# adaLN weight transfers held behind the weight stream, with other rates per stage, in a hybrid encoder block

## The chip, the cores and the metric

The kernel runs on one core of a Trainium2 chip. A core has a matrix engine (PE, with its weight loads shown apart as PEld), a vector engine (DVE), a scalar engine (ACT), a pool engine (POOL) and a sync engine (SP), and 16 DMA engines that move data between HBM and the on-chip memory. Every engine runs its own list of instructions in order, and waits at semaphores for the others. All transfers of this kernel are issued by SP. The metric is the device time of one execution in microseconds; smaller is better.

## The reference, cut to what matters

One layer works on a sequence of 256 tokens of width 2048, all in float32. A condition vector c makes nine modulation vectors (shift, scale and gate, three times), and three blocks follow: a SwiGLU FFN of inner width 5632, attention of 16 heads, and a second FFN.

```python
mod = jax.nn.silu(c) @ w_ada[l] + b_ada[l]
sh1, sc1, gt1, sh2, sc2, gt2, sh3, sc3, gt3 = jnp.split(mod, N_MOD, axis=-1)

f = swiglu(modulate(rms_norm(h, g_ffn1[l]), sh1, sc1), w1_gate[l], w1_up[l], w1_down[l])
h = h + 0.5 * gt1[:, None, :] * f

nrm = modulate(rms_norm(h, g_mix[l]), sh2, sc2)
qkv = nrm @ w_qkv[l]
...
mix = jnp.concatenate([o_na, o_dil], axis=-1) @ w_o[l]
h = h + gt2[:, None, :] * mix

f = swiglu(modulate(rms_norm(h, g_ffn2[l]), sh3, sc3), w2_gate[l], w2_up[l], w2_down[l])
h = h + 0.5 * gt3[:, None, :] * f
```

The adaLN matrix `w_ada` has 2048 x 18432 numbers, 151 MB, of the 500 MB that the kernel reads. It is only ever multiplied with one vector, so it doesn't go through the matrix engine.

## The kernel before

**The weight stream.** Every weight matrix of the FFNs and of attention lies in HBM as chunks of 128 x 1024 floats (512 KB), in the order in which they are used. `wraw` (L139) issues the transfer of one chunk into one of five `raw` buffers, and `wsplit` (L144) makes two halves of each float of it: ACT casts it to a short form, `hiw` (L147), and DVE subtracts that from the chunk, which gives `low` (L148). Each has four buffers. `mm2` (L151) then does two matmuls per 128 x 128 block, eight blocks to a chunk. `W.chunk` (L293) hands out the chunks, and keeps three more fetched and split ahead (AHEAD).

**The stages.** Inside an FFN the chunks are read in stages, named after the weights: `s` and `a` (a part of the up projection with the first rows of the input; `s` in the first FFN only), `b` (the rest of the up projection for 32 of 44 column blocks), `d` (the down projection of those), `c` (the up projection of the last 12 blocks), `e` (their down projection). The first FFN has 36, 80, 64, 48 and 24 chunks in a, b, d, c and e, attention has 96 for q, k and v and 32 for the output projection (units 0 to 127), and the second FFN 64, 64, 64, 48 and 24.

**The adaLN side stream.** Each of the 144 pieces of `w_ada` (16 for each of the nine vectors) is 128 x 2048 floats, 1 MB. `ada_issue` (L120) issues its transfer into one of two `ra` buffers or, during the FFNs, a third, `rx`; `ada_use` (L129) is one DVE multiply and sum over it (L132), which yields one column of a modulation vector `m`. They are needed at different times: vectors 0 and 1 by the first FFN's input, 2 as the gate of its output, 3 and 4 by attention's input, 5 by the output projection, 6 and 7 by the second FFN's input, 8 by its output. So they run beside the weight stream. `bg` lists what is still to be issued, `pend` what is issued and not used, and `bg_step` (L244) issues one and, when the buffers are full, uses the oldest first. With each chunk fetched, `W.chunk` adds the stage's rate to a credit (L297), and takes a step for each full point of it:

```python
self.credit += self.rate
while self.credit >= 1.0 and (bg or pend):
    self.credit -= 1.0
    if bg:
        bg_step()
```

`pace` (L315) sets the rate and clears the credit: RA for stage a of the first FFN, the four numbers of RB for b, d, c and e, RQ for attention, RE for stage a of the second FFN, RF for the rest. In some places everything must be done: `bg_until(0)` (L250) issues and uses all that is left. L402 does that after stage c and ahead of e, which begins at L403. 64 pieces (vectors 2, 4, 3, 5) are listed as stage b begins (L468).

**What sets the order.** The code above only says in which order the program is written. A planner then decides, ahead of time, the order in which each engine gets its instructions, from their dependencies and from the buffers that come free; an instruction written later can be put ahead of one written earlier, on SP too. Only the matmuls of attention keep their written order (L704). An order edge (`tc.add_manual_dep` with the class NoSync) makes the planner put one instruction behind another of the same engine; it puts no wait into the program. Before, one such edge exists, in `held` (L113): adaLN products written after a normalization stay behind the last instruction of it.

Of the kernel before, what the change touches and what calls it, by code (L numbers as in the profile page):

```python
# [36 lines left out]
QS = 1  # L37
PACT = 0
RA = 0.475
RB = (0.1, 0.5, 0.4, 0.15)  # L40
RQ = 0.33
RE = 0.25
RF = (0.1, 0.2, 0.1, 0.1)
AHEAD = 3
# [19 lines left out]
def build(tc, a):  # L64
    nc = tc.nc
    with ExitStack() as ctx:
# [43 lines left out]
        turn = [0]  # L110
        hold = []

        def held(ins):  # L113
            if hold:
                tc.add_manual_dep(
                    ins.ins, hold[-1].ins.name,
                    mybir.DependencyInfo(mybir.DependencyClass.NoSync, mybir.DependencyReason.DATA),
                    reason="hold")

        def ada_issue(i):  # L120
            turn[0] += 1
            if wide and turn[0] % (ARA + ARX) >= ARA:
                raw = wide["p"].tile([P, D], F32, tag="arx", bufs=ARX, name=f"rx{i}")
            else:
                raw = wp.tile([P, D], F32, tag="ara", bufs=ARA, name=f"ra{i}")
            nc.sync.dma_start(raw, a["w_ada"][i])
            return raw

        def ada_use(raw, i):  # L129
            j, k = i // KT, i % KT  # L130
            m = mods[j][:, k : k + 1]
            held(nc.vector.tensor_tensor_reduce(  # L132
                out=raw, in0=raw, in1=cb, scale=1.0, scalar=vec[:, BA + i : BA + i + 1],
                op0=ALU.mult, op1=ALU.add, accum_out=m))
            if j in GAIN:
                g = vec[:, GAIN[j] + k : GAIN[j] + k + 1]
                nc.vector.scalar_tensor_tensor(m, m, 1.0, g, ALU.add, ALU.mult)

        def wraw(src):  # L139
            raw = wp.tile([P, CW], F32, tag="raw", bufs=RAWB, name="rw")  # L140
            nc.sync.dma_start(raw, src)
            return raw

        def wsplit(raw):  # L144
# [99 lines left out]
        def bg_step():  # L244
            i, then = bg.pop(0)
            while len(pend) >= (ARA + ARX - 1 if wide else ARA - 1):
                bg_use()
            pend.append((ada_issue(i), i, then))
# [26 lines left out]
        class W:  # L275
# [8 lines left out]
            def fetch(self, n):  # L284
                while self.head < n:
                    self.ready[self.head] = wraw(srcs[self.head])
                    self.head += 1
# [5 lines left out]
            def chunk(self, ahead=AHEAD):  # L293
                while self.head <= min(self.tail + ahead, len(srcs) - 1):
                    self.ready[self.head] = wsplit(wraw(srcs[self.head]))
                    self.head += 1
# [5 lines that stand above are left out]
                        else:  # L302
                            bg_use()
                self.tail += 1
                return self.ready.pop(self.tail - 1)
# [13 lines left out]
        ws = W()  # L319
# [53 lines left out]
        def ffn(kx, part, ready_k, gate, rates, stat=None, out=None):  # L373


            hid = {}
            head = [pair("pb") for f in range(NF1)]
            ready_k(KM)
            for f in range(NF1):
                up_mm(head[f], kx, KM, True, False)  # L380
            ready_k(KT)
            ws.pace(rates[0])
            for f in range(NF1):
                up_mm(head[f], KM, KT, False, True)
                up_finish(f, head[f], part, hid)
            for f in range(NF1, F1):
                ps = pair("pb")
                up_mm(ps, kx, KT, True, True)
                up_finish(f, ps, part, hid)
            psum_pool("bank")  # L390
            ws.pace(rates[1])
            ffn_down(range(F1), hid, gate)
            psum_pool("pair")
            ws.pace(rates[2])
            for f in range(F1, FT):
                ps = pair("pb")
                up_mm(ps, 0, KT, True, True)
                up_finish(f, ps, {}, hid)
            ln_exp_set()
            psum_pool("bank")  # L400
            ws.pace(rates[3])
            bg_until(0)  # L402
            ffn_down(range(F1, FT), hid, gate, stat, out)  # L403
# [67 lines left out]
        def once(l, fn):  # L471
            def get(d):
                if (l, d) not in gates:
                    gates[l, d] = fn(d)
                return gates[l, d]
            return get
# [6 lines left out]

        ffn(K1, part, rest1, once(1, gate1), RB, stat=st)
        ws.pace(0.0)
# [10 lines left out]
        with tc.tile_pool(name="att", bufs=2) as ap_, tc.tile_pool(name="atc", bufs=1) as ac:  # L496
# [90 lines left out]
            def wo_unit(u, b, d):  # L587
                def fin(ps):
                    if b not in rows:
                        rows[b] = ost[b].rstd(8 * HD)  # L590
                    t = sp.tile([P, S], F32, tag="nt", name="wt")
                    nc.scalar.copy(t, ps[:, :S])
                    nc.vector.tensor_tensor(t, t, ps[:, S:], ALU.add)
                    nc.vector.scalar_tensor_tensor(t, t, mods[5][:, d : d + 1], rows[b], ALU.mult, ALU.mult)
                    nc.vector.tensor_tensor(h[d], h[d], t, ALU.add)
                    if b == 1:
                        hst.add(h[d])

                def last_fin(ps):
                    if d == KT - 1:  # L600
                        idle(9)
                    with tc.high_priority(offset=URGENT):
                        fin(ps)

                def go(whi, wlo):
                    ps = bank("pso")
                    for kk in range(8):
                        sl = slice(kk * P, (kk + 1) * P)
                        mm2(ps, whi[:, sl], wlo[:, sl], ox[b * 8 + kk], kk == 0, kk == 7)
                    at(u + (1 if d < KT - 1 else 0), lambda: last_fin(ps) if b == 1 and d >= KT - 2 else fin(ps))  # L610
                return go
# [88 lines left out]
            for b in range(2):  # L700
                for d in range(KT):
                    units.append(wo_unit(len(units), b, d))
            ws.pace(RQ)
            with tc.manual_schedule(engines=MANUAL):  # L704
# [127 lines left out]
def _program():  # L832
    import concourse.bacc as _bacc

    nc = _bacc.Bacc("TRN2", target_bir_lowering=False, num_devices=1, dynamic_dma_scratch_size=1024)
    aps = {k: nc.dram_tensor(f"in_{k}_dram", s, F32, kind="ExternalInput").ap() for k, s in _SHAPES.items()}
    aps["out"] = nc.dram_tensor("out_0_dram", (KT, P, S), F32, kind="ExternalOutput").ap()
    with tile.TileContext(nc) as tc:
        build(tc, aps)
    return nc  # L840
# [10 lines left out]
```

## Time and profile before

| | us |
|---|---|
| median of three runs | 1950.43 (1948.11 to 1951.84) |
| the profiled execution, its own time | 1961.22 |
| its span, first to last instruction | 1959.2 |
| one weight chunk, median from issue to landing, stage b / d | 5.0 / 4.1 |
| one adaLN piece, median from issue to landing | 7.6 |
| one adaLN product on DVE | 2.35 |
| one `low` on DVE | 1.22 |

The profile is of one execution. It gives for each engine what it did when, and for each time that it stood idle which other instruction or transfer ended the wait. A line such as `DVE low L148 <- ACT hiw L147` says that DVE, at line 148, making `low`, waited for ACT, which made `hiw` at line 147. SPq is the queue of SP, which issues the transfers; a chunk's transfer can be issued once `low` has been made from the chunk that lay in its buffer. "x3" after a merged row of the timeline counts the instructions in it. PEclk is the share of the full clock that was granted to the PE.

### The profile page before, as it was taken

Reading aid. Unit: us, or ns where it says so; the run is one execution under the profiler, and the core shown is the slowest. Engines: PE = TensorE matmul, PEld = TensorE weight load, DVE = VectorE, ACT = ScalarE, POOL = GpSimd, SP = SyncE. Lnnn points to the kernel's source line nnn. Section 1 sums busy time; section 2 is a strip of 40 time slices with the busy share of each in tenths; the row PEclk is TensorE's granted clock in tenths of the full one; section 3 lists DMA queues with packets and bytes.
Section 4 is the critical chain, followed back from the end, with each engine's and each line's share of the span. In section 5 each row is a group of like instructions: output and inputs, shape, how many; then the busy total and the mean of one; then the engine's idle time right before and its main releaser. Section 6 shows DMA issues by size and latency. Waiting matters only on the chain.

```text
span 1959.2 us, 27570 instructions
## 1 busy us (share of the span) xinstructions
PE 1916.7 (98%) x10564; PEld 1654.4 (84%) x10564; DVE 1568.9 (80%) x2122; ACT 906.5 (46%) x1333; POOL 0.7 (0%) x6
## 2 busy tenths in 40 slices
PE   7999999999999999999999999999999999999999
PEld 5878888888888888888888788888888888888887
DVE  7898999998788967989676899988899855555565
ACT  2444544433334454545555555444445433334442
POOL 0000000000000000000000000000000000000000
PEclk8999999999999999999999999999999999999999
DMA  9988889899989976698655545889876666666664
GB/s 380 374 325 299 314 308 312 302 328 334 344 319 324 336 247 192 235 339 302 205 170 162 158 144 189 310 321 328 321 241 192 190 186 185 189 186 184 188 197 130
DMA packets 120083, 503.98 MB, mean 257 GB/s; under 512 B 13328, under 2 KB 15632, under 8 KB 101520
## 3 DMA queue, kind: packets, MB, share of 16 engines
q1 hardware_dynamic: 119952, 502.24, 75.0%
q8 instruction: 82, 1.34, 0.3%
q14 instruction: 49, 0.40, 0.1%
HBM read 500.09 MB, written 2.10 MB: 256 GB/s over the span
## 4 chain that ended last, share of the span: by engine, by line
PE 87%; DVE 6%; DMA 3%; issue 2%; ACT 2%; SPq 0%; DVEq 0%; ACTq 0%
PE pb L153 22%; PE pd L153 15%; PE pb L154 11%; PE pa L153 9%; PE pd L154 8%; PE pa L154 4%; PE pqv L159 4%; PE pqk L159 4%; PE pso L153 2%; PE pa L452 2%; DVE low L148 2%; PE pqq L159 2%; DMA ra<-in_w_ada_dram 2%; PE pso L154 1%; DVE ra L132 1%
## 5 line engine op out<-in xcount | busy, mean ns | idle before, releaser
L147 ACT CAST hiw<-rw 128x1024 fp32r<-128x1024 f32 x644 | 674.8, 1051 | 776.0 <-PE pd L153 274.1
L148 DVE TENSOR_TENSOR low<-rw,hiw 128x1024 fp32r<-128x1024 f32 x644 | 783.7, 1223 | 238.5 <-ACT hiw L147 236.2
L153 PE MATMUL pb<-nx,hiw 128*128 128x512 f32 x1920 | 673.5, 395 | 0.0
L154 PE MATMUL pb<-nx,low 128*128 128x256 f32 x1920 | 539.8, 281 | 4.1 <-DVE low L148 4.1
L153 PE MATMUL pd<-hd,hiw 128*128 128x512 f32 x1408 | 493.7, 395 | 0.0
L153 PEld LDWEIGHTS pb<-nx,hiw 128*128 128x128 f32 x1920 | 360.7, 188 | 84.0
L154 PE MATMUL pd<-hd,low 128*128 128x256 f32 x1408 | 395.5, 281 | 2.0 <-DVE low L148 2.0
L154 PEld LDWEIGHTS pb<-nx,low 128*128 128x128 f32 x1920 | 363.8, 189 | 5.0 <-DVE low L148 5.0
L153 PEld LDWEIGHTS pd<-hd,hiw 128*128 128x128 f32 x1408 | 264.0, 188 | 62.0
L153 PE MATMUL pa<-nx,hiw 128*128 128x512 f32 x800 | 283.3, 399 | 3.6 <-ACT hiw L147 3.2
L132 DVE CUSTOM_DVE_ANT_0 ra<-ra,cb,vec 128x2048 f32<-128x2048 f32 x101 | 237.3, 2349 | 48.7 <-DMA ra<-in_w_ada_dram 48.5
L154 PEld LDWEIGHTS pd<-hd,low 128*128 128x128 f32 x1408 | 266.3, 189 | 3.0 <-DVE low L148 3.0
L154 PE MATMUL pa<-nx,low 128*128 128x256 f32 x800 | 224.1, 282 | 3.8 <-DVE low L148 3.8
L153 PEld LDWEIGHTS pa<-nx,hiw 128*128 128x128 f32 x800 | 149.6, 188 | 41.3 <-ACT hiw L147 5.2
L154 PEld LDWEIGHTS pa<-nx,low 128*128 128x128 f32 x800 | 151.2, 189 | 8.2 <-DVE low L148 7.1
L132 DVE CUSTOM_DVE_ANT_0 rx<-rx,cb,vec 128x2048 f32<-128x2048 f32 x43 | 101.0, 2349 | 19.7 <-DMA rx<-in_w_ada_dram 19.6
L153 PE MATMUL pso<-ox,hiw 128*128 128x512 f32 x256 | 91.5, 400 | 0.0
L159 PE MATMUL pqk<-hiw,nx 128*128 128x512 f32 x256 | 84.4, 395 | 0.0
L159 PE MATMUL pqq<-hiw,nx 128*128 128x512 f32 x256 | 83.0, 393 | 0.0
L159 PE MATMUL pqv<-hiw,nx 128*128 128x512 f32 x256 | 81.4, 392 | 0.3 <-ACT nx L222 0.3
L367 DVE SCALAR_TENSOR_TENSOR h<-pd,m,h 128x256 f32<-128x256 f32 x128 | 61.4, 483 | 24.1 <-PE pd L154 22.1
L154 PE MATMUL pso<-ox,low 128*128 128x256 f32 x256 | 72.1, 282 | 0.0
(133 smaller groups left out, 1510.9 us busy)
## 6 DMA issues: line engine op xcount, KB each, us to landing
ra<-in_w_ada_dram SPq DMA_DIRECT2D x101, 1024.0 KB, 7.6
rw<-in_w_b_dram SPq DMA_DIRECT2D x144, 512.0 KB, 5.0
rw<-in_w_d_dram SPq DMA_DIRECT2D x128, 512.0 KB, 4.1
rw<-in_w_a_dram SPq DMA_DIRECT2D x100, 512.0 KB, 5.1
rw<-in_w_c_dram SPq DMA_DIRECT2D x96, 512.0 KB, 4.0
rw<-in_w_qkv_dram SPq DMA_DIRECT2D x96, 512.0 KB, 4.2
rx<-in_w_ada_dram SPq DMA_DIRECT2D x43, 1024.0 KB, 7.6
rw<-in_w_e_dram SPq DMA_DIRECT2D x48, 512.0 KB, 4.2
```

The lines of the kernel that those rows point to most:

```text
L132: held(nc.vector.tensor_tensor_reduce(out=raw, in0=raw, in1=cb, scale=1.0, scalar=vec[:, BA + i : BA + i + 1], op0=ALU.mult, op1=ALU.add, ...
L147: nc.scalar.copy(hi, raw)
L148: nc.vector.tensor_tensor(lo, raw, hi.bitcast(F32), ALU.subtract)
L153: nc.tensor.matmul(out, lh, r, start=first, stop=False)
L154: nc.tensor.matmul(out[:, :S], ll, r[:, 0, :], start=False, stop=last)
L159: nc.tensor.matmul(out, l, r, start=first and i == 0, stop=last and i == 2, **kw)
L367: nc.vector.scalar_tensor_tensor(h[d], part_, g, h[d], ALU.mult, ALU.add)
L452: nc.tensor.matmul(pa[f][:, q, :], w[:, b * P : (b + 1) * P], full[k], start=k == 0 and q == 0, stop=k == K1 - 1 and q == 1, skip_group_ch ...
```

## The change

Three things are changed. `wraw` remembers the transfer that it issued last, in `queue`, while a rate is set. `ada_issue` puts an order edge from that weight transfer to its own, so that on SP an adaLN transfer can't come ahead of the weight transfer that is written ahead of it. And the rates of the first FFN's stages b, d, c and e, and of attention, are other numbers. The edge's helper, `after`, is taken out of `held`, which does what it did.

```diff
-RB = (0.1, 0.5, 0.4, 0.15)
-RQ = 0.33
+RB = (0.22, 0.35, 0.35, 0.3)
+RQ = 0.17
...
+        queue = []
+
+        def after(ins, other, why):
+            tc.add_manual_dep(
+                ins.ins, other.ins.name,
+                mybir.DependencyInfo(mybir.DependencyClass.NoSync, mybir.DependencyReason.DATA),
+                reason=why)
+
         def held(ins):
             if hold:
...
+                after(ins, hold[-1], "hold")
...
-            nc.sync.dma_start(raw, a["w_ada"][i])
+            ins = nc.sync.dma_start(raw, a["w_ada"][i])
+            if queue:
+                after(ins, queue[-1], "queue")
             return raw
...
             raw = wp.tile([P, CW], F32, tag="raw", bufs=RAWB, name="rw")
-            nc.sync.dma_start(raw, src)
+            ins = nc.sync.dma_start(raw, src)
+            if ws.rate:
+                queue[:] = [ins]
             return raw
```

The last rate of RB, that of stage e, meets an empty list before and after, since L402 has emptied it. In the lead-in (stage s) no rate is set, so no edge is made there.

More of the change, by code (lines that the diff above doesn't have):

```diff
@@ L111, in build @@
         hold = []
+        queue = []
[4 more added lines that the diff above has]
+                reason=why)
         def held(ins):
             if hold:
[L115 to L118, printed above, removed]
+                after(ins, hold[-1], "hold")
         def ada_issue(i):
```

## The prediction

> **What bounds the kernel now.** I read the page's busy shares, then a table of busy time by stage, then the waits, then the timeline of the two places where the PE stands still.
>
> ```profile
> PE 1916.7 (98%) x10564; PEld 1654.4 (84%) x10564; DVE 1568.9 (80%) x2122; ACT 906.5 (46%) x1333; POOL 0.7 (0%) x6
> ```
>
> The PE is the bound, with 42 us without a matmul in the whole span. The second fence is the busy table, one row a stage of the first FFN (a, b, d, c, e, named after the weights that they read), then attention with the output projection, then stage a of the second FFN. The bounds are the first matmuls of each stage. Columns: stretch, its length, busy us of each engine, granted clock, DMA share, GB/s.
>
> ```profile
> 68.00:179.20 111.20, 104.99 (x577) 87.89 (x577) 103.35 (x119) 51.98 (x69) 0.00 (x0) 1.00 0.90 336
> 179.20:402.20 223.00, 222.43 (x1282) 195.69 (x1281) 215.63 (x289) 109.50 (x146) 0.00 (x0) 1.00 0.87 304
> 402.20:583.10 180.90, 178.91 (x1027) 156.69 (x1026) 151.61 (x167) 68.30 (x67) 0.00 (x0) 1.00 0.91 331
> 583.10:721.50 138.40, 134.91 (x770) 118.63 (x769) 113.11 (x127) 62.28 (x81) 0.00 (x0) 0.99 0.89 316
> 721.50:788.30 66.80, 66.80 (x388) 58.96 (x387) 49.23 (x72) 33.43 (x44) 0.00 (x0) 1.00 0.61 190
> 788.30:1213.00 424.70, 412.69 (x2116) 349.28 (x2114) 353.72 (x630) 230.22 (x488) 0.00 (x0) 0.99 0.64 210
> 1213.00:1390.00 177.00, 176.84 (x1001) 153.54 (x1002) 156.68 (x170) 84.44 (x103) 0.00 (x0) 1.00 0.88 315
> ...
> 569.30 1.05 ACT L147 CAST hiw<-rw 128x1024 fp32r<-128x1024 f32 x1 [1.72 <-PE pd L153]
> 572.07 1.06 ACT L147 CAST hiw<-rw 128x1024 fp32r<-128x1024 f32 x1 [1.72 <-PE pd L153]
> ```
>
> The last two rows give the PE's own pace: ACT converts a chunk whenever the PE frees a buffer, and the two starts lie 2.77 us apart. At that pace stage a (36 chunks) would take 99.7 us, b (80) 221.6, d (64) 177.3, c (48) 133.0, e (24) 66.5. The table has 111.2, 223.0, 180.9, 138.4 and 66.8. So a loses 11.5, b 1.4, d 3.6, c 5.4, e 0.3. Stage a of the second FFN (64 chunks) loses nothing.
>
> Who is late? The waits of the PE in d and c, and the place in c:
>
> ```profile
> PE pb L154 <- DVE low L148: 3.5, 1, 3.5
> PE pd L154 <- DVE low L148: 2.0, 3, 0.9
> ...
> 589.45 2.35 DVE L132 CUSTOM_DVE_ANT_0 ra<-ra,cb,vec 128x2048 f32<-128x2048 f32 x1 [0.92 <-DMA ra<-in_w_ada_dram]
> 597.27 2.35 DVE L132 CUSTOM_DVE_ANT_0 rx<-rx,cb,vec 128x2048 f32<-128x2048 f32 x1 [4.32 <-DMA rx<-in_w_ada_dram]
> 599.55 1.22 DVE L148 TENSOR_TENSOR low<-rw,hiw 128x1024 fp32r<-128x1024 f32 x1
> ...
> 588.55 0.43 SPq L126 DMA_DIRECT2D rx<-in_w_ada_dram  x1
> 589.02 0.42 SPq L126 DMA_DIRECT2D ra<-in_w_ada_dram  x1
> 593.35 1.37 SPq L126 DMA_DIRECT2D ra<-in_w_ada_dram  x1
> ...
> 600.00:610.00 10.00, 9.18 (x44) 7.97 (x45) 10.00 (x12) 1.36 (x2) 0.00 (x0) 0.83 0.77 236
> ```
>
> Both stalls end at `low`, which DVE makes. In c, DVE stood 4.32 us before an adaLN product whose transfer had not landed, with `low` queued behind it; SP had issued three 1 MB transfers in 5 us. The granted clock of 0.83 over the next 10 us takes another 1.7 us. In d it is the same engine without a wait: at 402 to 411 us two products of 2.35 us stand between the last rows of stage b's epilogue:
>
> ```profile
> 402.20 2.35 DVE L132 CUSTOM_DVE_ANT_0 ra<-ra,cb,vec 128x2048 f32<-128x2048 f32 x1
> 407.88 2.35 DVE L132 CUSTOM_DVE_ANT_0 ra<-ra,cb,vec 128x2048 f32<-128x2048 f32 x1
> ```
>
> **The change part by part.** It adds and removes no instruction; it moves adaLN transfers on SP, and with them their DVE products. How far they stand from the program's own place now is seen from SP's timeline, in stage a and in stage b:
>
> ```profile
> 96.74 0.43 SPq L126 DMA_DIRECT2D ra<-in_w_ada_dram  x1
> 98.49 5.34 SPq L141 DMA_DIRECT2D rw<-in_w_a_dram  x2
> 103.88 0.43 SPq L126 DMA_DIRECT2D ra<-in_w_ada_dram  x1
> ...
> 279.72 0.33 SPq L126 DMA_DIRECT2D ra<-in_w_ada_dram  x1
> 282.75 3.23 SPq L141 DMA_DIRECT2D rw<-in_w_b_dram  x3
> 288.87 0.33 SPq L126 DMA_DIRECT2D rx<-in_w_ada_dram  x1
> ```
>
> In a there is one per two weight transfers, which is the rate 0.475: nothing is hoisted, RA stays, so the edge changes nothing there, and the 11.5 us stay. In b there is one per three although the rate says one per ten: the planner pulls them ahead of their place. The edge forbids that, so from here on the new rates are what runs.
>
> Counting the credit (L297): the 64 transfers of the layer are now written 7 in b (74 chunks at 0.1), 32 in d, 19 in c and 6 in the drain of L402. With the edge and the new rates: 16 (74 x 0.22), 22 (64 x 0.35), 16 (48 x 0.35) and 10 in the drain. What ran before, from the same busy table for tiles ra and rx (their products alone):
>
> ```profile
> 179.20:402.20 223.00, 32.88 (x14) 1.00 0.87 304
> 402.20:583.10 180.90, 42.31 (x18) 1.00 0.91 331
> 583.10:721.50 138.40, 25.86 (x11) 0.99 0.89 316
> ...
> 179.20:402.20 223.00, 18.78 (x8) 1.00 0.87 304
> 402.20:583.10 180.90, 21.17 (x9) 1.00 0.91 331
> 583.10:721.50 138.40, 11.76 (x5) 0.99 0.89 316
> ```
>
> That is 22 in b, 27 in d, 16 in c, none in e.
>
> Stage b: six products fewer, 14 us of DVE less; its 215.6 of 223 busy falls to about 201, so DVE no longer enters d late, and in d one transfer per 2.9 chunks replaces the pile at its start. The stall there is worth between 0 (the same epilogue still meets a product) and 3.6; I take 2.5, nearer to the top, because the second FFN makes its changes of stage without loss. Stage c: as many as before, one per 2.9 chunks instead of three in 5 us; between 0 and 5.4, I take 4.5. Sum of gains 7.0.
>
> Stage e gets 10 transfers and 12 products (two were pending), 12 x 2.35 = 28.2 us. With its own 49.2 that makes 77.4 in a stage of 66.5: 10.9 over. The lead of `low` over the PE, three chunks of the four buffers (8.3 us), covers most; 2.6 remain. That assumes that DVE doesn't wait for the transfers. Rows for both ends: in b, where DVE is full, the whole list of DVE's waits (200 to 400 us) has three entries and no DMA, its first below; in d DVE waited for adaLN transfers 25.0 us over 27 products, 0.93 each.
>
> ```profile
> DVE pt L340 <- PE pb L154: 1.0, 3, 0.6
> ...
> DVE ra L132 <- DMA ra<-in_w_ada_dram: 15.3, 10, 3.0
> DVE rx L132 <- DMA rx<-in_w_ada_dram: 9.7, 7, 2.2
> ...
> DVE ra L132 <- DMA ra<-in_w_ada_dram: 48.5, 35, 3.4
> DVE rx L132 <- DMA rx<-in_w_ada_dram: 19.6, 13, 4.3
> ```
>
> So e costs between 0 (products that run in c's slack) and 2.6 + 12 x 0.93 + 1.7 of clock = 15.5. I take 2.6: e is full like b. Behind a waiting product stand `low` and the update of h on DVE, and behind an adaLN issue on SP the weight transfers of e and qkv, which `low` releases.
>
> Attention: RQ halves from 0.33 to 0.17. Of its 16 transfers SP now issues 14 between units 15 and 49 and two already in c; tied, they go out between units 9 and 97. The stretch where they stand now loses 2.5 us on the PE, but the later stretches have stalls of the same kind without any:
>
> ```profile
> 900.00:950.00 50.00, 47.48 (x231) 39.38 (x231) 42.13 (x73) 27.37 (x71) 0.00 (x0) 1.00 0.78 276
> 1100.00:1150.00 50.00, 45.93 (x288) 40.74 (x287) 49.03 (x112) 28.73 (x60) 0.00 (x0) 1.00 0.51 155
> ```
>
> Between a gain of 2.5 and a loss of 2.5 (as many products, each a chance to stand before a softmax step); I take 0. RE and RF stay, the second FFN loses nothing now, and one transfer per four chunks or fewer asks less than now: 0.
>
> Sum against the profiled execution (span 1959.2, run 1961.2): -7.0 + 2.6 = -4.4 us. The median of the runs, 1950.4, lies 0.55% lower; I take the same difference there: **1946.0**.
>
> The Trainium skill, page "DMA: Bandwidth & Descriptors", section "Rules for kernel authors", speaks against this change: issue a DMA early, compute, and wait for its semaphore late. By it, an edge that holds transfers back lengthens DVE's waits; it is the last rival below. The trace agrees only in part: in b, where the transfers were pulled ahead furthest, DVE waited for none, yet the pulled-ahead ones in c met a 4.32 us wait.
>
> **The rivals.**
> 1. Nothing moves (the stalls stay at the changes of stage because the epilogue and a product meet there whatever the rate, or what is gained in d and c is paid in e): 1950. For it: d's stall had no DMA wait in it. Against: the second FFN has none.
> 2. All that is tied to adaLN goes: 1.4 + 3.6 + 5.4 + 2.5 = 12.9, with e free: 1937.5. Against: e's sum.
> 3. The drain at L402 makes DVE the bound of e: at d's wait of 0.93 the price is 15.5, the net +8.5: 1958.9. It decides from a mean wait of 0.69 us per product on (2.6 + 12 x 0.69 = 10.9, the gain of 7.0 and 3.9 more). For it: ten come due at once, with three buffers to land in. Against: b's list of waits.
> 4. Later issue, later landing everywhere: each product waits as the 48 that waited do now, 68.1/48 = 1.42 us. In c the room is (133.0 - 75.5 - 16 x 2.35)/16 = 1.24 us per product (75.5 is 113.11 less its products), so no gain survives there, and e pays 2.6 + 12 x 1.42 = 19.6: 1970.0.
>
> **How the numbers follow.** Forecast 0.46, rival 1 0.22, rival 2 0.11, rival 3 0.17, rival 4 0.04. The forecast's own range is 1941.4 (all 9.0 of d and c, e free) to 1949.5. A measurement of this kernel tells about 0.2% (3.9 us) from no change: faster is below 1946.5. Of the forecast's 0.46 some 0.34 lie there and 0.12 within; with rival 2 faster has 0.45, with rival 1 same has 0.34, slower 0.21. The range 1937 to 1959 leaves out rival 4 and parts of 2 and 3, and takes in the bounds of e.
>
> **What would show it.** Right: SP's rows in b show one adaLN issue per four or five weight transfers, in d and c per three; b's DVE falls to about 201 us; d and c take about 178 and 134 us; no slow clock at 600 us; some ten adaLN issues between the eighth last chunk of c and the end of e, e at 67 to 70 us. Wrong: stage a changed (the edge does more than I think), e above 75 us, d and c as long as before, or PE idle time in attention above 15 us (12 now).

## The result, and the profile after

The changed kernel is slower: 1965.51 us median of ten runs (1957.0 to 1980.71), against 1951.13 of ten runs of the kernel before (1944.37 to 1955.61). The two medians lie 14.4 us apart. The ratio on record is 1.0058, with a 95% interval of 1.0032 to 1.0083, which is 6 to 16 us more. The profiled execution of it took 1964.22 us, its span is 1962.4.

The first view is again the busy table by stage, of the changed kernel: b, d, c and e of the first FFN, then attention with the output projection (columns as before). The bounds are the first matmuls of each stage in this execution.

```profile
177.60:400.60 223.00, 222.36 (x1282) 195.55 (x1281) 205.62 (x273) 108.83 (x146) 0.00 (x0) 1.00 0.77 267
400.60:578.10 177.50, 177.50 (x1026) 156.51 (x1025) 144.35 (x163) 68.65 (x68) 0.00 (x0) 1.00 0.88 324
578.10:711.20 133.10, 133.10 (x770) 117.36 (x769) 114.21 (x128) 63.18 (x81) 0.00 (x0) 1.00 0.88 325
711.20:796.00 84.80, 70.14 (x386) 60.16 (x385) 69.30 (x91) 33.37 (x43) 0.00 (x0) 0.90 0.76 256
803.00:1215.40 412.40, 402.38 (x2042) 339.86 (x2042) 343.04 (x610) 225.12 (x478) 0.00 (x0) 0.99 0.65 212
```

Stage d went from 180.9 to 177.5 us and c from 138.4 to 133.1: the PE is busy in every microsecond of both. Stage e went from 66.5 (its matmuls alone, 721.5 to 788.0) to 84.8. That is -3.4, -5.3 and +18.3, together +9.6 us from the start of b to the end of e. Attention is what it was (412.7 before, 412.4; the prediction's row of 424.7 starts where e ends and runs 5 us into the second FFN).

Why e is longer shows in four views of the changed kernel: the waits of the PE from 700 to 805 us, those of ACT in stage e, the timeline of SP around its start, and that of the PE around its wait. Lines have moved: `hiw` is made at L156, `low` at L157, SP issues adaLN pieces at L131 and weight chunks at L148.

```profile
PE pd L162 <- ACT hiw L156: 14.6, 1, 14.6
...
ACT hiw L156 <- DMA rw<-in_w_e_dram: 13.0, 4, 12.2
...
696.67 1.46 SPq L148 DMA_DIRECT2D rw<-in_w_e_dram  x2
698.18 0.89 SPq L131 DMA_DIRECT2D ra<-in_w_ada_dram  x2
702.42 0.33 SPq L131 DMA_DIRECT2D rx<-in_w_ada_dram  x1
708.60 4.07 SPq L131 DMA_DIRECT2D ra<-in_w_ada_dram  x2
716.35 0.33 SPq L131 DMA_DIRECT2D rx<-in_w_ada_dram  x1
718.96 2.94 SPq L131 DMA_DIRECT2D ra<-in_w_ada_dram  x2
724.18 0.33 SPq L131 DMA_DIRECT2D rx<-in_w_ada_dram  x1
726.45 0.33 SPq L131 DMA_DIRECT2D ra<-in_w_ada_dram  x1
726.87 46.55 SPq L148 DMA_DIRECT2D rw<-in_w_e_dram  x21
...
734.34 1.22 PE L162 MATMUL pd<-hd,hiw 128*128 128x512 f32 x2 [14.62 <-ACT hiw L156]
...
720.00:740.00 20.00, 5.62 (x19) 4.38 (x20) 17.84 (x18) 5.53 (x6) 0.00 (x0) 0.57 1.01 399
```

The drain of L402 (L411 now) stands on SP as one row of ten adaLN transfers, with no weight chunk between them, from 698.2 to 726.9 us. Three buffers take them in, so each of the later ones waits until a product has freed one, and everything behind it on SP waits too. ACT then waits 12.2 us for the fourth chunk of e, and the PE behind it 14.6 us in one piece. The last row, the busy table from 720 to 740 us, shows the granted clock at 0.57 and the DMA engines full at 399 GB/s. The wait can be added up: the PE ran dry 21.54 us after the row began (at 719.72, which is 734.34 less its wait of 14.62) and went on 7.47 us after it ended, when the first chunk behind it had landed and been cast, and 28.69 - 21.54 + 7.47 = 14.62. The other 3.7 of the 18.3 us are matmuls that took longer (the PE is busy for 70.1 us where it was 66.5): about 2.5 at the lowered clock until 739, and about 1 at a slower pace of the PE after it, which the last section shows.

The two profiled spans differ by only 3.2 us, though b to e cost 9.6: the lead-in was 1.6 us shorter, and the second FFN 4.4 us (747.4 before, 743.0 after), which is the pace of the PE again (the faster one from 1735 us on in the changed kernel, the slower one throughout before); both paces occur with the edge and without it. In the tables below the losses of d and c are taken against their chunks at the pace of that run, 2.773 or 2.827 us a chunk, and those of e against 66.5.

### The profile page after: what moved, and what is told of

Its sections match the earlier page's. It is cut to its first block, busy times and chain, and to the rows that moved or that the text cites. A ratio compares the mean times of both kernels' runs of the same rounds, so it can differ in the third digit from the quotient of the medians.

```text
span 1962.4 us, 27572 instructions
## 1 busy us (share of the span) xinstructions
PE 1912.5 (97%) x10564; PEld 1652.4 (84%) x10564; DVE 1571.4 (80%) x2122; ACT 908.5 (46%) x1333; POOL 0.7 (0%) x6
## 4 chain that ended last, share of the span: by engine, by line
PE 83%; DVE 8%; DMA 4%; ACT 2%; issue 2%; SPq 0%; DVEq 0%; ACTq 0%
PE pb L162 21%; PE pd L162 16%; PE pb L163 11%; PE pd L163 8%; PE pa L162 8%; PE pa L163 4%; DMA ra<-in_w_ada_dram 4%; PE pqv L168 3%; DVE low L157 3%; PE pqk L168 3%; PE pso L162 2%; PE pa L461 2%; DVE ra L139 2%; PE pso L163 1%; ACT hiw L156 1%
## 5 line engine op out<-in xcount | busy, mean ns | idle before, releaser
L156 ACT CAST hiw<-rw 128x1024 fp32r<-128x1024 f32 x644 | 676.0, 1052 | 780.8 <-PE pd L162 261.9
L157 DVE TENSOR_TENSOR low<-rw,hiw 128x1024 fp32r<-128x1024 f32 x644 | 783.5, 1222 | 233.7 <-ACT hiw L156 231.7
L162 PE MATMUL pd<-hd,hiw 128*128 128x512 f32 x1408 | 494.2, 395 | 14.6 <-ACT hiw L156 14.6
L162 PEld LDWEIGHTS pd<-hd,hiw 128*128 128x128 f32 x1408 | 264.7, 188 | 76.3 <-ACT hiw L156 14.9
L168 PE MATMUL pqv<-hiw,nx 128*128 128x512 f32 x256 | 81.4, 392 | 0.3 <-ACT nx L231 0.3
```

Source lines behind the costliest of these rows:

```text
L156: nc.scalar.copy(hi, raw)
L157: nc.vector.tensor_tensor(lo, raw, hi.bitcast(F32), ALU.subtract)
L162: nc.tensor.matmul(out, lh, r, start=first, stop=False)
L168: nc.tensor.matmul(out, l, r, start=first and i == 0, stop=last and i == 2, **kw)
```

## The experiments

Theory Q: the row of adaLN issues keeps the weights of e off SP's queue, and the PE runs dry. Rival D, which the prediction had as its third: the drain's products make DVE the bound of e. Two more questions are which part of the change did what, and whether attention's rate matters.

**The edge alone.** The rates are those of before.

```diff
-RB = (0.22, 0.35, 0.35, 0.3)
-RQ = 0.17
+RB = (0.1, 0.5, 0.4, 0.15)
+RQ = 0.33
```

> The order edge alone, with the old rates (RB 0.1, 0.5, 0.4, 0.15; RQ 0.33). The drain ahead of stage e then holds 7 adaLN transfers instead of 10, and stage d issues one per two weight chunks. Theory Q (the row of adaLN issues on SP holds back the weights of e, and the PE runs dry): the stall grows by one product's 2.35 to 2.8 us per transfer once the PE's lead is used, so e takes 84.8 - 3 x 2.7 = about 77 us. Rival D (12 products make DVE the bound of e): 9 products are 7 us less DVE work, e at about 78 us; the two don't differ here. Both: d is the test of the rates; at one per two chunks DVE has 88 + 32 x 2.35 = 163 of 177 us of work, d between 177.5 and 181. Run time above before by 2 to 10 us.

Measured: ratio to before 1.0055 (1.0021 to 1.0089). The busy table of e, and the PE's waits from 395 to 805 us:

```profile
717.70:801.30 83.60, 70.51 (x385) 60.37 (x384) 67.15 (x88) 34.26 (x44) 0.00 (x0) 0.92 0.70 239
...
PE pd L162 <- ACT hiw L156: 13.1, 1, 13.1
PE pd L163 <- DVE low L157: 3.0, 1, 3.0
```

The edge by itself makes the kernel slower, in the same place. Stage d took 182.6 us, 5.1 over its pace: with the edge, the old 0.5 is really run there (31 products in d, 22 in the changed kernel), and near its start, at 415.9 us, a product waited 2.57 us for its transfer and the PE 3.0 us for the `low` behind it. The size of e was expected wrong: seven transfers cost 17.1 us, not some 10. SP's row lasted from 705.7 to 731.6 us, 25.9 us, nearly as long as the row of ten, and SP waited in it mostly for the products that free its buffers. Why seven take nearly as long as ten is not shown further; the other run with seven, below, has 24.9.

**The rates alone**, without the edge.

```diff
             ins = nc.sync.dma_start(raw, a["w_ada"][i])
-            if queue:
-                after(ins, queue[-1], "queue")
             return raw
```

> The new rates alone, without the order edge. Theory: without the edge the planner pulls the transfers ahead until buffers stop it, so rates below that do nothing: stages b, d, c and e as in the kernel before (223.0, 180.9, 138.4 and 66.5 us, each within 1 us), run time within 0.3% of before. Rival (the rates did the work in d and c): d at 177.5 and c at 133.1 us as in the changed kernel, with e above 70.

Measured: ratio 1.0012 (0.9976 to 1.0048). Stages d and c:

```profile
404.90:587.50 182.60, 181.70 (x1027) 156.79 (x1026) 153.50 (x166) 68.14 (x67) 0.00 (x0) 1.00 0.91 330
587.50:724.90 137.40, 136.08 (x771) 117.71 (x770) 111.31 (x127) 62.40 (x81) 0.00 (x0) 1.00 0.86 316
```

This execution ran its first FFN from b on at the slower pace, at which d and c take 180.9 and 135.7; so each still loses 1.7 us, with the PE idle in both, and e lost nothing (67.7 for 67.8). The stages missed the expected lengths by 1 to 4 us, mostly for the pace. The new rates without the edge do nothing that can be measured: up to attention every engine runs its instructions in the order of the kernel before, but for one pair on SP in stage b, so the transfers were pulled to the same places under both sets of rates. That tells one thing more: in this same order d and c lost 3.4 us here and 8.7 in the profile before (half a microsecond of it pace), so what these stalls cost differs from one execution to the next.

**The drain's products cut short**, with SP's order as in the changed kernel. This kernel leaves out most of the sum in twelve products. It ran once.

```diff
+            n = P if short[0] else D
             held(nc.vector.tensor_tensor_reduce(
-                out=raw, in0=raw, in1=cb, scale=1.0, ...
+                out=raw[:, :n], in0=raw[:, :n], in1=cb[:, :n], scale=1.0, ...
...
             ws.pace(rates[3])
+            short[0] = True
             bg_until(0)
+            short[0] = False
```

> The changed kernel, with the 12 products that the drain makes cut to the first 128 of 2048 columns (so part of the modulation vectors is left out): DVE has some 26 us less to do there, the order on SP and every transfer stay. Theory Q: ten transfers of 1 MB still stand ahead of e's weights; at 380 GB/s they take 27.6 us, about what they took (698 to 726 us), so the PE still runs dry: e at 76 to 85 us. Rival D: with the DVE work gone e takes 67 to 70 us.

Measured: e took 81.4 us. Its busy row, then the waits of SP from 690 to 760 us:

```profile
713.00:794.40 81.40, 68.95 (x385) 59.97 (x384) 51.32 (x86) 33.40 (x43) 0.00 (x0) 0.92 0.76 257
...
SPq L132 <- DMA ra<-in_w_ada_dram: 11.4, 5, 5.1
SPq L132 <- DMA rx<-in_w_ada_dram: 4.6, 3, 1.7
```

DVE has 18 us less to do in e (51.3 for 69.3) and the stage is only 3.4 us shorter, some 1 us of which is the pace after the stall. The row on SP still lasted 25.4 us; now it waits mostly for the landing of the transfers themselves. Rival D falls: DVE's work accounts for about 3 us of the row and not for the stall.

**The same ten transfers, spread over e.**

```diff
-RB = (0.22, 0.35, 0.35, 0.3)
+RB = (0.22, 0.35, 0.35, 0.5)
...
             ws.pace(rates[3])
-            bg_until(0)
```

> The changed kernel without the drain ahead of e, and with a rate of 0.5 in e: the same ten transfers now stand on SP one behind every second weight chunk of e, and the same products of 2.35 us are made in e. Theory Q: weights are never more than one transfer late, e at 66.5 to 70 us (DVE is over by 10.9 us less a lead of 8.3), and the whole about 7 us faster than before (d 177.5, c 133.1). Rival D: DVE is as full as in the changed kernel, e at 78 to 85 us, the whole not faster than before.

Measured: ratio 0.9974 (0.9939 to 1.0008), which can't be told from no change; 7 us less were expected. Stages d, c and e, then two rows of SP's timeline in e:

```profile
406.10:587.00 180.90, 180.90 (x1027) 156.80 (x1026) 144.64 (x163) 68.47 (x68) 0.00 (x0) 1.00 0.87 320
587.00:722.60 135.60, 135.60 (x770) 117.52 (x769) 113.09 (x127) 63.20 (x81) 0.00 (x0) 1.00 0.87 313
722.60:790.40 67.80, 67.80 (x386) 58.81 (x385) 65.74 (x90) 32.76 (x43) 0.00 (x0) 1.00 0.86 322
...
726.70 0.42 SPq L131 DMA_DIRECT2D rx<-in_w_ada_dram  x1
731.38 1.92 SPq L148 DMA_DIRECT2D rw<-in_w_e_dram  x2
```

All three stages are at the (slower) pace to a tenth of a microsecond: the same ten transfers, with nine products in the stage as in the changed kernel and DVE busy 65.7 of 67.8 us, cost it nothing when two weight chunks stand between each two. After e, 3.2 us were lost ahead of attention; for 2.3 of them the PE waited for DVE's last square of the norm. So the position on SP is the cause, not the amount of work or of bytes. No run issues the weights from another engine's queue, so how much the full DMA engines alone would have cost beside such a row isn't shown.

**Fewer and more in the row.** One rate of RB, that of c, leaves seven or fourteen transfers for the drain. Each ran once.

```diff
-RB = (0.22, 0.35, 0.35, 0.3)
+RB = (0.22, 0.35, 0.42, 0.3)
...
-RB = (0.22, 0.35, 0.35, 0.3)
+RB = (0.22, 0.35, 0.27, 0.3)
```

> The changed kernel with 0.42 instead of 0.35 in c, so that the drain holds 7 transfers instead of 10. Theory Q with a lead: ten transfers kept e's weights off SP for 28.7 us (698.1 to 726.9) and cost 17.3 at the PE's faster pace, so the lead was 11.4 us; seven cost 7 x 2.87 - 11.4 = 8.7, e at 75 us. Rival (what counts is that a drain is there, as the edge alone seemed to show, where 7 cost 17): e at 82 to 85 us.

> The changed kernel with 0.27 instead of 0.35 in c, so that the drain holds 14 transfers, with one weight chunk between the fourth and the fifth. Theory Q: 14 x 2.87 - 11.4 - 2.8 = about 26, e at 90 to 95 us. Rival (a drain costs the same whatever its length): 82 to 85 us.

Measured: e took 78.4 and 99.3 us. The busy rows of e and the PE's waits, first with seven, then with fourteen:

```profile
722.90:801.30 78.40, 69.08 (x386) 59.50 (x385) 64.36 (x86) 33.40 (x43) 0.00 (x0) 0.93 0.74 245
...
PE pd L162 <- ACT hiw L156: 9.3, 1, 9.3
```

```profile
716.60:815.90 99.30, 71.25 (x385) 60.92 (x384) 79.30 (x99) 33.30 (x43) 0.00 (x0) 0.83 0.75 255
...
PE pd L162 <- ACT hiw L156: 24.7, 1, 24.7
PE pd L163 <- DVE low L157: 3.3, 1, 3.3
```

The cost grows with the row (11.9, 18.3 and 32.8 us above 66.5 for 7, 10 and 14), so a drain is not a fixed price. Both were expected too small, since they counted 2.87 us a transfer. The time for which the row keeps weights off SP does better: 24.9 us for seven (708.9 to 733.8), 28.7 for ten, 45.1 for fourteen (703.7 to 748.9, with one chunk between), 25.9 in the run of the edge alone and 25.4 with short products. Less what e lost, that leaves 13.0, 10.4, 12.3, 8.8 and 10.5 us. This remainder, nine to thirteen us in each of the five, is what the weight stream's lead covered, less the landing of the first chunk behind the row and the slower matmuls; what moves it within these bounds isn't shown.

**Nothing left for the drain.** This and the next run were made to beat both kernels.

```diff
-RB = (0.22, 0.35, 0.35, 0.3)
+RB = (0.28, 0.38, 0.45, 0.3)
```

> The order edge with rates that leave nothing for the drain (RB 0.28, 0.38, 0.45): all of the layer's adaLN transfers stand between weight chunks of b, d and c. Theory Q: no stall in e, none in d and c as long as their rates stay below one per two chunks; at the PE's faster pace d takes 177.5, c 133.1 and e 66.5 us, 9 us less than in the kernel before; run time 0.3 to 0.6% under before. Rival (an edge costs wherever rates are this high): c at 0.45 loses 3 us or more, as before.

Measured: 1946.82 us median, beside 1955.57 of the kernel before on the same chip; ratio 0.9957 (0.9932 to 0.9982). Stages d, c and e:

```profile
401.70:579.20 177.50, 177.50 (x1027) 156.51 (x1026) 147.40 (x161) 68.61 (x67) 0.00 (x0) 1.00 0.91 335
579.20:712.30 133.10, 133.10 (x771) 117.36 (x770) 119.26 (x133) 61.83 (x80) 0.00 (x0) 1.00 0.91 338
712.30:778.70 66.40, 66.40 (x385) 58.57 (x384) 50.12 (x73) 34.17 (x44) 0.00 (x0) 1.00 0.64 200
```

The stall of e is gone and the gains of d and c stay. The edge, which alone made the kernel slower, is worth 0.4% once the rates of b, d and c add up to the 64 pieces that must be through before e (20, 24 and 21 by the credit). This version is faster than both kernels.

**The same, with attention's rate of before.**

```diff
-RQ = 0.17
+RQ = 0.33
```

> As the run that leaves nothing for the drain, with RQ back at 0.33. Theory: halving RQ moved nothing that the PE waits for; attention with the output projection takes 412 to 414 us from the first v matmul to the second FFN, and the run time is the same within 0.2%. Rival: the halved rate relieved DVE in attention, and 0.33 costs 2 to 3 us there.

Measured: 1946.98 us, ratio 0.9957 (0.9929 to 0.9985). Attention with the output projection took 411.4 us, against 414.0 in the run before it, 412.7 in the kernel before and 412.4 in the changed one. In the run time the halved rate neither helps nor harms.

## Why the prediction was wrong

**Right:** that stage a doesn't change, since its transfers already stood where the edge puts them; that without the edge the rates aren't what runs; the counts per stage, to about one, and the ten in the drain; that the stalls of d and c go; that attention and the second FFN give nothing. The price of d and c also came out (7.0 us were taken, 8.7 came, out of a stated 9.0), but with luck in it: it was read from one execution, and the same order lost only 3.4 us in the run of the rates alone. DVE's time in b fell to 205.6 us, where 201 was stated. One reading was off: the longest of d's three waits, 0.9 us, did stand behind a product that waited for its transfer (0.77 us, at 443.4).

**Wrong:** the step "e costs between 0 and 15.5, I take 2.6". It measured 18.3, beyond its upper end, and turned -4.4 into a loss. The step counted DVE's work against the length of the stage and the lead of `low`. Its sentence on the queue, that behind an adaLN issue on SP stand the weight transfers of e, was there, but without a price: it took for granted that the ten would mix with e's weights as they had in b. In b they mixed because adaLN pieces written later were pulled between weights written earlier. In the drain all ten are written ahead of e's fourth chunk, and the weights were not moved ahead of them. What had to be counted was the row itself: 10.5 MB at the 380 GB/s that the page of the kernel before shows for its first slice give 27.6 us without a weight chunk, where SP took 28.7, against the prediction's lead of `low` of 8.3 us. Row less lead is 19 to 20 us, near the measured 18.3; that sum was not made. It is a rough one: the 18.3 are a wait of 14.6 and 3.7 us of slower matmuls.

**The rivals.** The third named the place and nearly the size (15.5 for 18.3, with the kernel at 1958.9 for a measured 1965.5), but not the mechanism: its condition, a mean wait of DVE above 0.69 us per product, did not hold, since DVE waited for adaLN transfers only 1.7 us in all from 690 to 800 us, by the first two rows below; and with the products cut short e was still 14.9 us over. The first (nothing moves) is what the rates alone do. The second needed a free e. The fourth had the numbers that lie nearest, 19.6 us for e and 1970.0, but by chance: its condition, a longer wait at every product, fell most clearly. It rested on the rule of the Trainium skill, page "DMA: Bandwidth & Descriptors", section "Rules for kernel authors", that a DMA is best issued early. Here the tied transfers were issued later, and DVE waited less for them: in d and c 14.6 us, by the last two rows below, from 400 to 711 us of the changed kernel, against 25.0 in d alone before. Why they waited less isn't shown.

```profile
DVE ra L139 <- DMA ra<-in_w_ada_dram: 1.2, 4, 0.4
DVE rx L139 <- DMA rx<-in_w_ada_dram: 0.5, 2, 0.3
...
DVE ra L139 <- DMA ra<-in_w_ada_dram: 11.2, 11, 3.0
DVE rx L139 <- DMA rx<-in_w_ada_dram: 3.4, 5, 1.4
```

The range (1937 to 1959) missed because its upper end was rival 3, with e at 15.5 us less the gains of d and c. With the 18.3 and 8.7 of the profiles the same sum gives 1960.0. The median measured is 5.5 us above that; the profiled execution doesn't show where those are, and the interval of the ratio holds both.

## What to carry to other kernels

An order edge that keeps a side stream in its place also takes away the planner's means to mend a wrong rate: before it, two sets of rates ran in the same order, and after it the rates must add up, or what is left meets the next point where everything must be done. When transfers are moved to such a point, count what stands in one row on the issuing queue, how long it lasts (bytes and, where buffers turn around, the engine that frees them), and hold it against the lead of the stream behind it; that sum is separate from whether the engines have the time. Spread by one transfer per two chunks, the same work cost the stage nothing, and with nothing left for the drain the kernel was 0.4% faster than before.

## What the runs showed of the hardware that was not expected

The PE runs the same sequence of matmuls at two paces, both at a granted clock of 1.00. Two stretches of the timeline of the PE in the changed kernel, in the second FFN:

```profile
1599.97 0.28 PE L163 MATMUL pd<-hd,low 128*128 128x256 f32 x1
1600.09 0.40 PE L162 MATMUL pd<-hd,hiw 128*128 128x512 f32 x1
1600.33 0.28 PE L163 MATMUL pd<-hd,low 128*128 128x256 f32 x1
...
1799.97 0.28 PE L163 MATMUL pb<-nx,low 128*128 128x256 f32 x1
1800.09 0.39 PE L162 MATMUL pb<-nx,hiw 128*128 128x512 f32 x1
1800.32 0.28 PE L163 MATMUL pb<-nx,low 128*128 128x256 f32 x1
```

A pair takes 0.36 us in the first (1599.97 to 1600.33) and 0.35 in the second; over 16 matmuls, one chunk, it is 2.827 and 2.773 us, 1.9% apart, and each pace mostly holds for hundreds of microseconds. Stage b of the second FFN (64 chunks) took 180.9 us in four of the ten profiles of this study and 177.5 in the other six, with the edge and without it. The pace sometimes changed after the PE had stood still (at the stall of e in the changed kernel, at the start of d before, there for some 33 us only) and twice in the middle of a stage at a single pair that took a little longer: 0.56 us at 1734 us of the changed kernel, and 0.39 us at 1665 us of the run with the short products, for 0.35 or 0.36 around it. The nine stages of the FFNs from b of the first on, 480 chunks, differ by 25.6 us between all slow and all fast, which is about the spread of the runs of one kernel (1942.88 to 1970.51 us in 25 runs of the kernel before on one chip); that the spread comes from there isn't shown. The prediction counted the slower pace of the second FFN as no loss (its row of 177.0 leaves out that stage's first 5 us), and half a microsecond of d's 3.6 was of this kind. What sets the pace stayed open: no run was made to tell.
